# Values of four heads at once, with 512 columns, and output projections inside the recurrence

## The chip, the cores and the metric

The kernel runs on one core of a Trainium2 chip. The metric is the device time of one execution in microseconds (us). Five engines work beside each other, each through its own list of instructions in order: TensorE (PE in the profile; its weight loads PEld), VectorE (DVE), ScalarE (ACT), GpSimd (POOL) and SyncE (SP), which here only issues DMAs. An instruction that waits holds up all that stand behind it on its engine.

## The reference: what is computed

Two layers over 512 latent tokens of width 1024, with 256 context tokens. Layer 0 is a gated linear recurrence in both directions over 16 heads; layer 1 is a convolution module, which the change doesn't touch. In layer 0, cut down:

```
p = h @ w_in                       # 1024 x 10240, for latents h and context hc
q, v, zf, zb, gate = split(p, 5)
gf, kf = log f, 1 - f   with f = lb + (1 - lb) * sigmoid(zf)       # the same for zb
sc = state after the context, from (kc, vc, gc)                    # per direction
S_t = diag(exp g_t) S_(t-1) + k_t^T v_t ;  o_t = S_t^T q_t         # per head, chunks of 16
y  = (rmsnorm(o_forward + o_backward) * silu(gate)) @ w_out
x  = x + gate_ada * y,   where shift, scale, gate_ada = split(silu(c) @ ada_w + ada_b, 3)
```

All is float32. The large products are made as three products of split numbers (a high part rounded to fp32r and the rest): high by high, low by high, high by low.

## The kernel before

After an opening that makes the modulated inputs `h_hi`, `h_lo` (and `hc` for the context), layer 0 runs over eight pairs of heads, `gi` = 0 to 7 (L607). A pair projects its forget gates (`proj_z`, tiles pz for the latents, pc for the context, weights wz), its queries (`proj_silu`, pq, wq), its values (`proj_values`, pv, wv) and its gates (pg, wg), and, in the pairs that `OUT_SETS` names (L42), adds the output projection of finished heads to the stream (`out_proj`, tiles op, weights wo). Then come the pair's two heads: `gla` (L321) makes the decays, the state S and the scores, up to the output o, and `readout` (L527) normalises and gates it. `gla` is a generator: its first part ends behind the state updates (L424, L427), its second at the output products (L517 to L525). After a pair come some of 32 pieces of the ada product (`ada_piece`, L161; the table in L685 gives each pair 4, 4, 4, 3, 3, 3, 3 and none): a piece is one load `adb` and eight VectorE instructions that sum into `adacc`, and a small matmul `adbps`.

The order on each engine is made by a scheduler from the program's order, the dependences and the free buffers of the pools, so products of the next pair stand among the steps of the heads of the pair before.

Weights come through `wpiece` (L196): SP loads 512 KB into a tile with the tag `raw`, ScalarE makes the high half (tag `whi`), VectorE the low half (`wlo`). `ada_piece` takes its `adb` from the same tag `raw`. The pool has three buffers of it (`wpool`, L75), so a load waits until the third load before it has been used up by both engines. PSUM tiles of products (`pj`) have three buffers.

The values of a pair take 2 weight pieces of 4 x 256, then for each of 6 token tiles (4 of latents, 2 of context) 24 matmuls of 256 columns (L304, L305, L308) and one copy to SBUF by ScalarE (L603). The last pair (`gi` = 7) has an order of its own (L624 to L637) and ends with the output projections of heads 10 to 13 and of heads 14 and 15.

## Time and profile before

| | us |
|---|---|
| median of 3 timed runs | 1325.85 (1321.75 to 1326.63) |
| profiled execution | 1325.56, span 1323.5 |
| mean granted TensorE clock | 0.991 |
| TensorE busy | 1288.8 (97%) |
| VectorE busy | 934.4 (71%) |
| ScalarE busy | 608.2 (46%) |
| GpSimd busy | 304.3 (23%) |
| memory traffic | 120.22 MB, 91 GB/s |

Busy time is the time in which an engine has an instruction under way; matmuls overlap, so the mean length of one (284 ns for one with 256 columns) is more than the distance from one to the next. The granted clock is a share of 2.4 GHz; at 0.50 TensorE runs at 1.2 GHz. A row in which an instruction ends with x8 holds eight of them. Names of tiles have their numbers left out, so h_o is any head's output.

### The profile page before, as it was taken

How to read it: one execution, taken by the hardware profiler on the slowest of the kernel's cores; microseconds unless marked ns; L12 is line 12 of the kernel's file. 1: busy time of each engine (PE TensorE's matmuls, PEld its weight loads, DVE VectorE, ACT ScalarE, POOL GpSimd, SP SyncE). 2: the span in 40 equal slices, each digit the busy share in tenths (PEclk: the TensorE clock that was granted, in tenths of full speed). 3: DMA queues.
4: the chain of work that ended last, by engine and by line, in shares of the span. 5: the costliest groups of instructions: out<-in, count | busy, mean ns of one | idle time of the engine just before them, and what ended most of it. 6: DMA issues, size and time to landing. Idle time of an engine off the chain costs nothing.

```text
span 1323.5 us, 19786 instructions
## 1 busy us (share of the span) xinstructions
PE 1288.8 (97%) x7956; PEld 1087.4 (82%) x7956; DVE 934.4 (71%) x1513; ACT 608.2 (46%) x920; POOL 304.3 (23%) x289
## 2 busy tenths in 40 slices
PE   6999999999999999999999999999999999999997
PEld 2698898888889888889889889876877778788887
DVE  6667987796787888687689788865666576574233
ACT  4355564552464354565256455524423233385331
POOL 2231330330231151151024033104212112112121
PEclk8999999999999999999999999999999999999999
DMA  9322113114112312213311311213433333123321
GB/s 352 156 80 79 51 49 128 49 49 159 54 47 77 128 49 77 84 49 97 112 36 62 122 39 48 75 48 108 135 103 122 120 96 119 64 80 96 96 80 64
DMA packets 36188, 120.22 MB, mean 91 GB/s; under 512 B 4643, under 2 KB 7107, under 8 KB 36097
## 3 DMA queue, kind: packets, MB, share of 16 engines
q1 hardware_dynamic: 35104, 115.79, 26.0%
q0 software_dynamic: 992, 3.18, 1.1%
q8 instruction: 62, 1.02, 0.3%
q14 instruction: 30, 0.24, 0.1%
HBM read 116.85 MB, written 2.10 MB: 90 GB/s over the span
## 4 chain that ended last, share of the span: by engine, by line
PE 77%; DVE 13%; ACT 4%; DMA 3%; issue 2%; POOL 1%; SPq 0%; DVEq 0%; ACTq 0%
PE pa L734 4%; PE pa L735 4%; PE pa L739 4%; PE pz L293 3%; PE pz L294 3%; PE pz L296 3%; PE op L563 2%; PE cop L876 2%; PE cop L880 2%; PE op L565 2%; PE op L564 2%; PE cop L877 2%; PE pgt L803 2%; PE pgt L801 2%; PE pgt L800 2%; PE py L773 2%
## 5 line engine op out<-in xcount | busy, mean ns | idle before, releaser
L734 PE MATMUL pa<-ci_hi,h_hi 128*128 128x512 f32 x256 | 100.3, 403 | 1.9 <-ACT h_hi L682 1.9
L735 PE MATMUL pa<-ci_lo,h_hi 128*128 128x512 f32 x256 | 99.7, 393 | 0.0
L293 PE MATMUL pz<-h_hi,wz_hi 128*128 128x512 f32 x232 | 92.1, 397 | 1.4 <-ACT wz_hi L136 1.4
L294 PE MATMUL pz<-h_lo,wz_hi 128*128 128x512 f32 x232 | 91.7, 395 | 0.0
L116 POOL TENSOR_SCALAR sg<-sg 128x1536 f32<-128x1536 f32 x16 | 75.6, 4726 | 63.6 <-ACT sg L582 63.3
L167 DVE SCALAR_TENSOR_TENSOR adacc<-adb,sc,adacc 128x128 f32<-128x128 f32 x224 | 76.9, 357 | 3.8
L424 DVE SCALAR_TENSOR_TENSOR h_S<-h_S,h_dec,h_kb 128x128 f32<-128x128 f32 x96 | 59.0, 614 | 27.1 <-ACT h_kb L418 26.0
L136 ACT ACTIVATE ci_hi<-ci_raw 128x1024 fp32r<-128x1024 f32 x29 | 30.8, 1061 | 102.2 <-PE pa L739 57.9
L138 POOL TENSOR_TENSOR ci_lo<-ci_raw,ci_hi 128x1024 fp32r<-128x1024 f32 x18 | 44.2, 2461 | 129.2 <-ACT ci_hi L136 102.9
L739 PE MATMUL pa<-ci_hi,h_lo 128*128 128x512 f32 x224 | 70.9, 392 | 0.0
L510 POOL TENSOR_TENSOR h_A<-a,a 128x512 f32<-128x512 f32 x16 | 36.6, 2290 | 129.8 <-DVE a L491 108.0
L304 PE MATMUL pv<-wv_hi,h_hi 128*128 128x256 f32 x256 | 63.3, 284 | 0.0
L305 PE MATMUL pv<-wv_hi,h_lo 128*128 128x256 f32 x256 | 63.3, 284 | 0.0
L296 PE MATMUL pz<-h_hi,wz_lo 128*128 128x512 f32 x232 | 60.7, 396 | 0.0
L734 PEld LDWEIGHTS pa<-ci_hi,h_hi 128*128 128x128 f32 x256 | 48.7, 190 | 14.1 <-issue 4.1
L136 ACT ACTIVATE wz_hi<-wz_raw 128x1024 fp32r<-128x1024 f32 x29 | 30.7, 1057 | 63.6 <-DMA wz_raw<-in_w_in 54.7
L294 PE MATMUL pc<-hc,wz_hi 128*128 128x256 f32 x232 | 59.1, 288 | 0.0
L293 PE MATMUL pc<-hc,wz_hi 128*128 128x256 f32 x232 | 58.8, 287 | 0.0
L735 PEld LDWEIGHTS pa<-ci_lo,h_hi 128*128 128x128 f32 x256 | 48.7, 190 | 11.5 <-issue 1.4
L138 DVE TENSOR_TENSOR wz_lo<-wz_raw,wz_hi 128x1024 fp32r<-128x1024 f32 x29 | 35.5, 1223 | 31.1 <-ACT wz_hi L136 30.7
L876 PE MATMUL cop<-zhi,co_hi 128*128 128x512 f32 (+1 forms) x160 | 54.2, 352 | 0.0
L369 POOL TENSOR_TENSOR h_ref<-h_tot,h_gt 128x64 f32<-128x64 f32 x16 | 16.8, 1048 | 160.5 <-DVE h_ref L396 157.3
(332 smaller groups left out, 3862.1 us busy)
## 6 DMA issues: line engine op xcount, KB each, us to landing
adb<-in_ada_c SPq DMA_DIRECT2D x32, 512.0 KB, 3.2
ci_raw<-in_c_in SPq DMA_DIRECT2D x32, 512.0 KB, 3.2
wz_raw<-in_w_in SPq DMA_DIRECT2D x29, 512.0 KB, 3.2
ada<-in_ada_a SPq DMA_DIRECT2D x16, 512.0 KB, 10.2
wv_raw<-in_w_v SPq DMA_DIRECT2D x16, 512.0 KB, 3.2
wg_raw<-in_w_in SPq DMA_DIRECT2D x16, 512.0 KB, 3.2
cg_raw<-in_c_gate SPq DMA_DIRECT2D x16, 512.0 KB, 3.2
co_raw<-in_c_out SPq DMA_DIRECT2D x16, 512.0 KB, 3.6
```

The source lines that it names most:

```text
L116: (G if pool_min else V).tensor_scalar(out=t, in0=t, scalar1=EMAX, scalar2=None, op0=ALU.min)
L138: lo_eng.tensor_tensor(out=lo, in0=raw, in1=hi.bitcast(F32), op=ALU.subtract)
L167: V.scalar_tensor_tensor(out=acc, in0=raw[:, k, :], scalar=sc[:, k, 0:1], in1=acc, op0=ALU.mult, op1=ALU.add)
L293: mm(ps[:, :T], lhsT=hi[:, k, :], rhs=rhi[k], start=(k == 0), stop=False)
L294: mm(ps[:, :T], lhsT=hi[:, k, :], rhs=rlo[k], start=False, stop=False)
L296: mm(ps[:, :T], lhsT=lo[:, k, :], rhs=rhi[k], start=False, stop=(k == KD - 1))
L304: mm(ps[:, :256], lhsT=lhi[k][:, c], rhs=hi[:, k % 4, :], start=(k == 0), stop=False)
L305: mm(ps[:, :256], lhsT=llo[k][:, c], rhs=hi[:, k % 4, :], start=False, stop=False)
L734: mm(pss[t], lhsT=h_hi[:, 2 * kq + k, c], rhs=hi[:, k, :], start=(kq == 0 and k == 0), stop=False)
L735: mm(pss[t], lhsT=h_hi[:, 2 * kq + k, c], rhs=lo[:, k, :], start=False, stop=False)
L739: mm(pss[t], lhsT=h_lo[:, 2 * kq + k, c], rhs=hi[:, k, :], start=False, stop=(kq == 3 and k == 1))
L876: mm(ps, lhsT=hi[:, i, c], rhs=zhi[ct][:, tok], start=(ct == 0), stop=False)
```

## The change

Values are made for four heads at a time: `proj_values(qi)` stands in the even pairs only, loads 4 weight pieces of 2 x 512, makes for each of the 6 token tiles 24 matmuls of 512 columns (the context's tiles first, and the three products of a k block next to each other), and copies each PSUM tile out in two halves of 256 columns, one to the value tile of each of the two pairs. The gates (pg) are projected ahead of the values. The output projections now cover heads 0 to 3, 4 to 7 and 8 to 11 in the pairs 2, 4 and 6, written after the first part of the pair's first head instead of ahead of its heads; in the last pair heads 12 and 13 remain, then 14 and 15 as before. Copies of the split weights get 4 buffers instead of 3 (`W_BUFS`), of which the opening uses one more. The layout of w_v changes on the host's side of the inputs, and the program's scratch for dynamic DMAs is set to 8192. The number of output products (384), of their weight loads (20) and of the value weights' loads (16 of 512 KB) is what it was. Lines of the changed kernel stand one or two off from those of the kernel before.

```diff
--- before.py
+++ after.py
@@ -37,9 +37,10 @@
 RX_BUFS, RX_ENG, WE_ENG = 3, (0, 0, 1, 0, 0, 1, 0, 0), (1, 1, 0, 0, 0)
 CTX_MOD = ((), (), (0, 1, 2, 3, 4, 5), (6, 7))
 LAST_KQ = 1
+W_BUFS = 4
 FINAL = ((0, 2, 1), (2, 4, 0), (4, 6, 0))
 SET_LN_EXP, SET_SILU = 6, 18
-OUT_SETS = {2: (0, 1, 2, 3), 3: (4, 5), 5: (6, 7, 8, 9)}
+OUT_SETS = {2: (0, 1, 2, 3), 4: (4, 5, 6, 7), 6: (8, 9, 10, 11)}
 
 C_RESET = 0
 C_PRE = C_RESET + L
@@ -196,7 +197,7 @@
     def wpiece(src, shape, name, lo_eng, hi_eng=None):
         raw = wpool.tile([P] + shape, F32, name=f"{name}_raw", tag="raw")
         nc.sync.dma_start(out=raw, in_=src)
-        return split(wpool, raw, shape, name, lo_eng, ("whi", "wlo"), 3, hi_eng)
+        return split(wpool, raw, shape, name, lo_eng, ("whi", "wlo"), W_BUFS, hi_eng)
 
 
     with l0:
@@ -254,7 +255,7 @@
                     V.tensor_tensor(out=t, in0=x_sb[:, k, :], in1=rs, op=ALU.mult)
                     modulate(t, k, mod_g[:, k, 0:1], mod_s[:, k, 0:1], hx_hi, hx_lo)
                 for i in range(len(early), min(EARLY, len(early) + EARLY_LOADS[jj])):
-                    pool, tags, bufs = (wpool, ("whi", "wlo"), 3) if i < 3 else (pi, ("ehi", "elo"), EARLY - 3)
+                    pool, tags, bufs = (wpool, ("whi", "wlo"), W_BUFS) if i < W_BUFS else (pi, ("ehi", "elo"), EARLY - W_BUFS)
                     w = split(pool, wraws[i], [KD, P], f"we{i}", (V, G)[WE_ENG[i]], tags, bufs)
                     pspool, tag = (ps_p, "pj") if i < 3 else (ps_s, "sc")
                     early.append((w, pspool.tile([P, 512], F32, name=f"pe{i}", tag=tag)))
@@ -300,12 +301,10 @@
             ps = ps_p.tile([P, 512], F32, name=name, tag="pj")
             c = slice(t * P, (t + 1) * P)
             for k in range(KD):
-                hi, lo = ws[k // 4]
-                mm(ps[:, :256], lhsT=lhi[k][:, c], rhs=hi[:, k % 4, :], start=(k == 0), stop=False)
-                mm(ps[:, :256], lhsT=llo[k][:, c], rhs=hi[:, k % 4, :], start=False, stop=False)
-            for k in range(KD):
-                hi, lo = ws[k // 4]
-                mm(ps[:, :256], lhsT=lhi[k][:, c], rhs=lo[:, k % 4, :], start=False, stop=(k == KD - 1))
+                hi, lo = ws[k // 2]
+                mm(ps, lhsT=lhi[k][:, c], rhs=hi[:, k % 2, :], start=(k == 0), stop=False)
+                mm(ps, lhsT=llo[k][:, c], rhs=hi[:, k % 2, :], start=False, stop=False)
+                mm(ps, lhsT=lhi[k][:, c], rhs=lo[:, k % 2, :], start=False, stop=(k == KD - 1))
             return ps
 
         def silu_of(ps, t, name):
@@ -592,16 +591,18 @@
             silu_of(ps, t, f"{tag}{gi}_{j}")
             return t
 
-        def proj_values(gi):
-            ws = [wpiece(w_v[gi, kh], [4, 256], f"wv{gi}_{kh}", V) for kh in range(2)]
-            v = pt.tile([P, 6, 256], F32, name=f"v{gi}", tag="v", bufs=2)
-            for t in range(6):
+        def proj_values(qi):
+
+            ws = [wpiece(w_v[qi, kq], [2, 512], f"wv{qi}_{kq}", V) for kq in range(4)]
+            vs = [pt.tile([P, 6, 256], F32, name=f"v{qi}_{i}", tag="v", bufs=2) for i in range(2)]
+            for t in (4, 5, 0, 1, 2, 3):
                 if t < NB:
-                    ps = proj_v(ws, hx_hi, hx_lo, t, f"pv{gi}_{t}")
+                    ps = proj_v(ws, hx_hi, hx_lo, t, f"pv{qi}_{t}")
                 else:
-                    ps = proj_v(ws, hc_hi, hc_lo, t - NB, f"pv{gi}_{t}")
-                act(out=v[:, t, :], in_=ps[:, :256], func=AF.Copy)
-            return v
+                    ps = proj_v(ws, hc_hi, hc_lo, t - NB, f"pv{qi}_{t}")
+                for i in range(2):
+                    act(out=vs[i][:, t, :], in_=ps[:, i * 256:(i + 1) * 256], func=AF.Copy)
+            return vs
 
         m1 = cpool.tile([P, KD], F32, name="m1")
         for gi in range(8):
@@ -612,20 +613,22 @@
             if gi < 7:
                 sgs = [proj_z(gi, j) for j in range(2)]
                 qss = [proj_silu(0, gi, j, "q") for j in range(2)]
-                v = proj_values(gi)
                 gss = [proj_silu(4, gi, j, "g") for j in range(2)]
-                if gi in OUT_SETS:
-                    out_proj(OUT_SETS[gi])
+                if gi % 2 == 0:
+                    vs = proj_values(gi // 2)
+                v = vs[gi % 2]
                 for j in range(2):
                     parts = gla(h + j, j, sgs[j], qss[j], v)
                     next(parts)
+                    if j == 0 and gi in OUT_SETS:
+                        out_proj(OUT_SETS[gi])
                     readout(h + j, next(parts), gss[j])
             else:
                 sg, qs = [], []
                 for j in range(2):
                     sg.append(proj_z(gi, j))
                     qs.append(proj_silu(0, gi, j, "q"))
-                v = proj_values(gi)
+                v = vs[1]
                 parts = [gla(h + j, j, sg[j], qs[j], v) for j in range(2)]
                 next(parts[0])
                 next(parts[1])
@@ -634,7 +637,7 @@
                 readout(h, po, gs[0])
                 po = next(parts[1])
                 readout(h + 1, po, gs[1])
-                out_proj([10, 11, 12, 13])
+                out_proj([12, 13])
 
                 xg = [pt.tile([P, 3, L], F32, name=f"xg{i}", tag="sg", bufs=2) for i in range(2)]
                 xg = [xg[k // 3][:, k % 3, :] for k in range(6)]
@@ -938,7 +941,7 @@
     d["ada_c"] = np.concatenate([ada_w[0][:, 2 * D:], ada_w[1]], axis=1).reshape(KD, P, 32, P).transpose(2, 1, 0, 3)
     d["lb_logits"] = hgrn_lb_logits[:, 0].reshape(2, NH, P).transpose(2, 0, 1)
     d["w_in"] = hgrn_w_in[0].reshape(KD, P, 5, 8, 2, P).transpose(2, 3, 4, 1, 0, 5)
-    d["w_v"] = hgrn_w_in[0][:, E2:2 * E2].reshape(2, 4, P, 8, 256).transpose(3, 0, 2, 1, 4)
+    d["w_v"] = hgrn_w_in[0][:, E2:2 * E2].reshape(4, 2, P, 4, 512).transpose(3, 0, 2, 1, 4)
     d["hnorm_g"] = hgrn_norm_g[0].reshape(P, 1)
     d["w_out"] = hgrn_w_out[0].reshape(NH, P, 4, 256).transpose(2, 1, 0, 3)
     ci = conv_w_in[0].reshape(4, 2, P, 3, 4, 512)
@@ -957,7 +960,7 @@
     from concourse.bass_utils import run_bass_kernel_spmd as _run
 
     arrays = {f"in_{k}": v for k, v in _layout(**{k: np.asarray(v) for k, v in inputs.items()}).items()}
-    nc = _bacc.Bacc("TRN2", target_bir_lowering=False, num_devices=1)
+    nc = _bacc.Bacc("TRN2", target_bir_lowering=False, num_devices=1, dynamic_dma_scratch_size=8192)
     args = [nc.dram_tensor(k, v.shape, mybir.dt.from_np(v.dtype), kind="ExternalInput").ap() for k, v in arrays.items()]
     args.append(nc.dram_tensor("out_0", (P, KD, L), F32, kind="ExternalOutput").ap())
     with tile.TileContext(nc, schedule_with_timeline_sim=True) as tc:
```

The first place is TensorE before the first product of pair 2 (pz2_00, with the weights wz2_00). In these names pv1_5 is the last value tile of pair 1, pg1_0 and pg1_1 are pair 1's gates, adbps an ada piece's sum, and h2_ the small steps of head 2. Before:

```order
L308 MATMUL pv1_5_1834<-wv1_0_lo_1695,hc0_111 128x256 x4
L308 MATMUL pv1_5_1834<-wv1_1_lo_1701,hc1_112 128x256 x4
L293 MATMUL pg1_0_1866<-h_hi_81,wg1_0_hi_1862 128x512
...
L296 MATMUL pg1_1_1904<-h_hi_81,wg1_1_lo_1902 128x512 x8
L346 MATMUL h2_ct_1952<-kc_85,h2_ec_1944 128x128 x4
...
L413 MATMUL h2_kt0_2000<-kc_85,h2_kb_1993 128x128 x3
...
L293 MATMUL pz2_00_2369<-h_hi_81,wz2_00_hi_2365 128x512
```

The pair's value products stand ahead of its gates, and behind head 1's output. In the changed kernel the same place reads:

```order
L523 MATMUL h1_o_1316<-h1_qh_1214,h1_S_1181 128x128 x2
L294 MATMUL pg1_0_1716<-h_hi_81,wg1_0_hi_1712 128x512
...
L297 MATMUL pg1_1_1754<-h_hi_81,wg1_1_lo_1752 128x512 x8
L170 MATMUL adbps1_1369<-ones_94,adacc1_1360 128x1
L170 MATMUL adbps2_1383<-ones_94,adacc2_1374 128x1
L474 MATMUL h2_s0d_1890<-h2_qh_1841,h2_kl0_1888 64x64 x8
...
L170 MATMUL adbps3_1397<-ones_94,adacc3_1388 128x1
L345 MATMUL h2_ct_1802<-kc_85,h2_ec_1794 128x128 x4
...
L416 MATMUL h2_pp0_1855<-v0_1_811,h2_kb_1843 128x128 x3
L412 MATMUL h2_kt1_1863<-kc_85,h2_kb_1843 128x128 x3
L294 MATMUL pz2_00_2219<-h_hi_81,wz2_00_hi_2215 128x512
```

No value products are left between head 1's output and pz2_00: only the gates' products and head 2's small ones. The second place is VectorE at the end of ada piece 5 (adacc5), whose load stands three loads ahead of wz2_00's. Here wz2_00_lo is the low half of those weights, gs1_ are pair 1's gates, a1_0 the scores that the masked copies fill, and h3_ec belongs to head 3. Before:

```order
L165 TENSOR_SCALAR adacc5_2322<-adb5_2320,sc_100 128x128
L167 SCALAR_TENSOR_TENSOR adacc5_2322<-adb5_2320,sc_100,adacc5_2322 128x128 x4
L317 TENSOR_TENSOR gs1_0_1891<-gs1_0_1891,g1_0_e_1892 128x512
L167 SCALAR_TENSOR_TENSOR adacc5_2322<-adb5_2320,sc_100,adacc5_2322 128x128 x3
L313 TENSOR_SCALAR gs1_1_1929<-pg1_1_1904 128x512
L440 TENSOR_TENSOR h2_kl0_2038<-h2_kh_1992,h2_f16_1986 128x512
L336 SCALAR_TENSOR_TENSOR h3_ec_2129<-ones_94,h3_gt_2124 128x255
L338 SCALAR_TENSOR_TENSOR h3_ec_2129<-ones_94,h3_gt_2124 128x255
L138 TENSOR_TENSOR wz2_00_lo_2367<-wz2_00_raw_2363,wz2_00_hi_2365 128x1024
L491 COPY_PREDICATED a1_0_116<-masks_115,h2_s0d_2040 64x4x64 x2
```

and in the changed kernel:

```order
L312 TENSOR_SCALAR gs1_1_1779<-pg1_1_1754 128x512
...
L439 TENSOR_TENSOR h2_kl0_1888<-h2_kh_1842,h2_f16_1836 128x512
...
L490 COPY_PREDICATED a1_0_116<-masks_115,h2_s0d_1890 64x4x64 x2
...
L166 TENSOR_SCALAR adacc5_2172<-adb5_2170,sc_100 128x128
L168 SCALAR_TENSOR_TENSOR adacc5_2172<-adb5_2170,sc_100,adacc5_2172 128x128 x2
L457 COPY_PREDICATED a1_0_116<-masks_115,h2_sx_1892 128x512
L168 SCALAR_TENSOR_TENSOR adacc5_2172<-adb5_2170,sc_100,adacc5_2172 128x128 x5
L335 SCALAR_TENSOR_TENSOR h3_ec_1979<-ones_94,h3_gt_1974 128x255
L337 SCALAR_TENSOR_TENSOR h3_ec_1979<-ones_94,h3_gt_1974 128x255
L341 SCALAR_TENSOR_TENSOR h3_ec_1979<-sg1_1_1517,h3_ec_1979 128x512
L139 TENSOR_TENSOR wz2_00_lo_2217<-wz2_00_raw_2213,wz2_00_hi_2215 128x1024
```

Steps of head 2 that stood behind ada piece 5 (the copies into a1_0, the gate gs1_1 and kl0) now stand ahead of its end. From head 1's last state update to the end of the piece the list has 61 instructions before and 71 in the changed kernel; to the end of ada piece 12 behind head 5 it has 66 there, and to that of ada piece 18 behind head 9 it has 62. On SP the third place reads, in the changed kernel:

```order
L164 DMA adb4_2156<-in_ada_c 128x1024
L164 DMA adb5_2170<-in_ada_c 128x1024
L164 DMA adb6_2184<-in_ada_c 128x1024
L164 DMA adb7_2198<-in_ada_c 128x1024
L199 DMA wz2_00_raw_2213<-in_w_in 128x1024
L199 DMA wz2_10_raw_2271<-in_w_in 128x1024
...
L199 DMA wg2_1_raw_2560<-in_w_in 128x1024
L199 DMA wv1_0_raw_2598<-in_w_v 128x1024
```

The pieces adb4 to adb7 stand ahead of wz2_00 as they did before; the value weights (wv1 holds heads 4 to 7) moved behind the gates' weights.

## Rows read from the trace of the kernel before

**Rows 1.** The page: busy time by engine; granted clock in 40 slices.
```profile
PE 1288.8 (97%) x7956; PEld 1087.4 (82%) x7956; DVE 934.4 (71%) x1513; ACT 608.2 (46%) x920; POOL 304.3 (23%) x289
...
PEclk8999999999999999999999999999999999999999
```

**Rows 2.** Windows between two heads' last output products, columns in the first line.
```profile
core 0: us, PE busy (x) PEld busy (x) DVE busy (x) ACT busy (x) POOL busy (x), PEclk, DMA share, GB/s
185.60:237.40 51.80, 51.11 (x394) 46.22 (x394) 42.41 (x87) 23.24 (x40) 6.81 (x13) 1.00 0.28 92
394.40:462.00 67.60, 67.60 (x472) 59.53 (x471) 53.85 (x104) 30.80 (x51) 6.80 (x13) 1.00 0.31 102
597.40:675.70 78.30, 78.30 (x532) 69.40 (x530) 54.50 (x95) 31.73 (x49) 7.28 (x13) 1.00 0.29 95
809.70:876.40 66.70, 66.26 (x453) 60.69 (x452) 53.18 (x92) 32.12 (x55) 9.44 (x13) 1.00 0.17 52
```

**Rows 3.** Timeline of DVE (start, length, instruction): head 1's state, ada piece 5.
```profile
181.19 0.34 DVE L424 SCALAR_TENSOR_TENSOR h_S<-h_S,h_dec,h_kb 128x128 f32<-128x128 f32 x1
...
210.51 1.12 DVE L167 SCALAR_TENSOR_TENSOR adacc<-adb,sc,adacc 128x128 f32<-128x128 f32 x3
```

**Rows 4.** Chain of waits (start, length, what): products, a weight load.
```profile
188.07 0.96 PE pv L308 x8
...
205.33 1.81 PE pg L296 x8
...
217.64 3.20 DMA wz_raw<-in_w_in
```

**Rows 5.** Timeline of ACT: the high half of pair 2's first weights.
```profile
215.15 1.05 ACT L136 ACTIVATE wz_hi<-wz_raw 128x1024 fp32r<-128x1024 f32 x1
```

**Rows 6.** Timeline of PE: head 1's output, first product of wz2_00.
```profile
185.30 0.61 PE L524 MATMUL h_o<-h_qh,h_S 128*128 128x128 f32 x4
...
217.79 0.50 PE L293 MATMUL pz<-h_hi,wz_hi 128*128 128x512 f32 x1
```

**Rows 7.** Groups of value products: count | busy us, mean ns | idle before.
```profile
L304 PE MATMUL pv<-wv_hi,h_hi 128*128 128x256 f32 x256 | 63.3, 284 | 0.0
...
L304 PE MATMUL pv<-wv_hi,hc 128*128 128x256 f32 x128 | 31.7, 284 | 0.0
```

**Rows 8.** Window of the value tiles alone: length, PE, PEld, ACT busy.
```profile
185.60:217.80 32.20, 15.48 (x122) 14.94 (x122) 2.28 (x6) 1.00 0.30 99
```

**Rows 9.** Groups by line and form on DVE, columns as in rows 7.
```profile
L450 DVE TENSOR_TENSOR h_kl<-h_kh,h_fac 128x256 f32<-128x256 f32 x64 | 26.0, 463 | 0.0
...
L491 DVE COPY_PREDICATED a<-masks,h_s0d 64x256 f32<-64x256 uint8 x56 | 24.8, 444 | 6.4 <-PE h_s0d L475 5.1
...
L138 DVE TENSOR_TENSOR wg_lo<-wg_raw,wg_hi 128x1024 fp32r<-128x1024 f32 x16 | 19.5, 1217 | 0.9 <-PE pv L308 0.7
...
L440 DVE TENSOR_TENSOR h_kl<-h_kh,h_f 128x512 f32<-128x512 f32 x16 | 13.9, 871 | 0.0
...
L317 DVE TENSOR_TENSOR gs<-gs,g_e 128x512 f32<-128x512 f32 x16 | 11.0, 690 | 6.2 <-ACT g_e L316 6.2
L313 DVE TENSOR_SCALAR gs<-pg 128x512 f32<-128x512 f32 x16 | 10.9, 684 | 9.3 <-PE pg L296 9.2
...
L458 DVE COPY_PREDICATED a<-masks,h_sx 128x512 f32<-128x512 uint8 x14 | 10.4, 742 | 0.9
```

**Rows 10.** Window of PE alone, filled by head 2's small products.
```profile
212.60:217.80 5.20, 4.51 (x82) 1.00 0.30 101
```

**Rows 11.** Timeline of DVE: the last step of head 15's readout.
```profile
887.90 0.68 DVE L551 TENSOR_TENSOR h_ohl<-h_sq,h_ohl 128x512 fp32r<-128x512 f32 x1
```

**Rows 12.** Windows of PE in the opening: length, busy time, granted clock.
```profile
57.60:59.80 2.20, 0.37 (x2) 1.00 0.00 0
61.50:64.90 3.40, 3.37 (x8) 0.50 0.02 5
```

**Rows 13.** Waits of PE: us in total, times, longest.
```profile
PE pz L293 <- ACT wz_hi L136: 1.4, 1, 1.4
```

## The prediction

> **What bounds the kernel now.** I read the page's engine line first, then the windows between heads, then the chain of waits, and last single instructions around one boundary. TensorE is busy 1288.8 us of the 1323.5 us span, and its clock stands near full in nearly every slice [rows 1]; so work taken from TensorE shortens the run only where nothing else is late in its place. What nearly is late shows in the windows from the last output product of one head to that of the next: at heads 1 to 2, 5 to 6 and 9 to 10 TensorE is busy for 51.1 of 51.8, 67.6 of 67.6 and 78.3 of 78.3 us, while VectorE works 42.4, 53.9 and 54.5 us of the same stretches [rows 2]. VectorE is a second runner some 10 to 24 us behind, and the chain of waits already passes through it and the weight loads there.
>
> The link between the two is the `raw` buffers. Three of them serve all weight loads and the 32 ada pieces, and SP issues the loads in program order, ada pieces of a pair ahead of the next pair's first weights. Pair 2's first forget weights (wz2_00) therefore load only when VectorE has finished with ada piece 5. How close that is today: VectorE ends head 1's last state update at 181.53 and ada piece 5 at 211.63 [rows 3], 30.1 us later; the weights' load takes 3.2 us [rows 4] and their high half is ready at 216.20 [rows 5], 4.6 us behind the ada piece. TensorE, which ended head 1's output at 185.9, reaches the product that needs them at 217.79 [rows 6]: the weights are only 1.6 us early.
>
> **The change, part by part.** The sum stands against the profiled execution, 1325.56 us (span 1323.5; the median of the three timed runs is 1325.85, so both mean the same).
>
> *Value products.* Before: 1152 matmuls of 256 columns. The groups of 256 and of 128 in [rows 7] are the hi·hi ones, and the other two kinds have as many. Eight in a row take 0.96 us, 0.120 each; eight of 512 columns take 1.81 us, 0.226 each [rows 4]. After: 576 of 512 columns. 1152 x 0.120 = 138.2, 576 x 0.226 = 130.3: **-7.9**. If the denser window's mean for a value product, 15.48/122 = 0.127 [rows 8], held for all, the gain would be 16; if one of 512 columns cost two of 256, nothing. I take the two rows of eight, since they are runs of just these shapes. The Trainium skill, "TensorE: Matmul & The Clock Gate", section Back-to-back issue gap, gives an isolated gap of N/2.4 ns plus 2.5 ns; by it the whole saving would be an estimated 1.5 us, because wider products save only the fixed part. The rows' fixed part is larger than that, so the trace does not bear the formula out.
>
> *Where the values go.* They and the output projections are gone from the odd pairs, and it is in odd pairs that the three ada-gated loads come (pairs 1, 3 and 5 ahead of pairs 2, 4 and 6). The even pairs get the double.
>
> Boundary 1 to 2: of the 32.2 us from head 1's output to wz2_00's product, 122 value products go: 122 x 0.120 = 14.6 us [rows 8]. VectorE's list from the last state update to the end of ada piece 5 grows meanwhile from 61 to 71 instructions: more of head 2 is put ahead of the piece. Added are four kl of 0.463, four masked copies of 0.444, the two gate steps of 0.684 and 0.690, a kl of 0.871 and a masked copy of 0.742; two weight splits of 1.217 fall away [rows 9]: +4.2. So the wait is 14.6 - 1.6 + 4.2 = **17.2**. From the other side: 30.1 + 4.2 + 4.6 = 38.9 us after the state update the weights are there; TensorE has 4.4 us to head 1's end, 48 products of 512 columns (10.9) and head 2's small products (5.2 [rows 10]), 20.5 in all: 18.4. I keep 17.2.
>
> Boundary 5 to 6: the list to ada piece 12 has 66 instructions, and the mean of the stretch is 53.85/104 = 0.518 [rows 2]: 34.2, plus 4.6, is 38.8. TensorE has 4.4 + 87 x 0.226 + 5.2 = 29.3: **9.5**. Boundary 9 to 10: 62 x 54.50/95 (0.574) = 35.6, plus 4.6, is 40.2; TensorE 4.4 + 98 x 0.226 + 12 x 0.120 + 5.2 = 33.2: **7.0**. Together 33.7.
>
> That is the upper bound, since it lets VectorE's list keep the pace that it has now, idle time included or replaced by other work. The lower: VectorE idles 9.4 of 51.8, 13.8 of 67.6 and 23.8 of 78.3 us [rows 2]. If the lists of some 35 us close up by those shares, the weights come 6.4, 7.1 and 10.6 us sooner, and 10.8 + 2.4 + 0 = 13.2 us of waiting is left. Some of the idle is by TensorE's pace and goes (masked copies wait for products, [rows 9]); the rest is the head's own chain over ScalarE, which stays. I take **+28**, nearer the upper end, because 17.2 of it rests on a boundary where the slack was read directly.
>
> Even pairs: their stretches gain 15.3 us of values (144 x 0.226 - 144 x 0.120) and an output projection of 96 products (21.7 us). VectorE's work stays as it is, so TensorE stays last and no wait forms; what is queued there is in the sum already. The values need four weight pieces before the first product ends; the load behind them takes 3.2 us a piece against 24 products of 0.226 for a piece's share, so they are hidden: 0 (bounds 0 and 3 x 3.2).
>
> *Last pair.* In the last stretch (809.7 to 876.4) TensorE loses 144 value products (17.3 us) and half an output projection of 96 (48 x 0.226 = 10.8 us), VectorE has 53.2 of 66.7 us there [rows 2]. Head 15's readout then runs from 876.4 to 888.6 [rows 11]; the projection of heads 10 to 13 covers it today, and by the order about 5 us of the smaller one of heads 12 and 13 is left behind head 15's output. At most 12.2 - 5 = 7 is bare there, and another 3 in the stretch; at least 0, if the projection is late enough. **+4**.
>
> *Clock.* After a wait of 2.2 us TensorE's granted clock was 0.50, its 1.2 GHz level, for 3.4 us in which it did 8 products; later it is 1.00 again [rows 12]. Half of 3.4 is 1.7 lost. For the two longer waits: **+3.4** (0 to 5.1 with the third). The Trainium skill, same page, Part 1: The HAM clock gate, says that throttled is the default and activity releases it; that agrees with these rows, and would make every long wait cost more than its own length, as summed here.
>
> *Waits of before that go.* The one wait for wz_hi of 1.4 us [rows 13] lies where the even pair's products now stand: **-1.4** (0 to -1.4).
>
> *At nothing:* the 48 copies that bring values out of PSUM are as many and as wide as before (six took ScalarE 2.28 us, 0.38 each [rows 8]). A value tile's PSUM buffer is now held for two of them, 0.76 us, beside 24 products of 0.226 (5.4 us) into the next of three buffers: 0; bare, the second copies of 24 tiles would be 9.1. The fourth weight buffer can only let a split run earlier, and cannot let a load start, since `raw` still has three: 0 (0 to -3). The scratch size touches only POOL's DMA queue: 0 (plus or minus 1).
>
> Sum: -7.9 + 28 + 4 + 3.4 - 1.4 = **+26.1**, 1351.7: I say 1352.
>
> **Rivals.**
> *The waits don't come* (faster). Then only the values count: 1325.6 - 7.9 = 1318. For it: VectorE has time over in the lengthened even pairs and could run ahead of TensorE into the odd ones. Against: its list waits there for the head's own products and for `raw` buffers, and the odd pair's slack today is 1.6 us. Chance 0.08.
> *VectorE closes up:* waits 13.2, clock 1.7: 1325.6 - 7.9 + 13.2 + 4 + 1.7 - 1.4 = 1335. For it: its idle share [rows 2]. Chance 0.20.
> *The loads behind follow late too:* after the first weights each boundary waits once more for a load (3.2), since all pass the three `raw` buffers; with the upper waits, the last pair at 10 and the clock at 5.1: 1325.6 - 7.9 + 33.7 + 9.6 + 10 + 5.1 = 1376. Against: a piece's 24 and 24 products take 8.3 us, longer than load and split. Chance 0.14.
> *Forecast*, 0.58.
>
> **How the numbers follow.** The range takes the second rival in and ends just short of the third: 1332 to 1374. Within 0.5% (6.6 us, what a measurement of this kernel can tell) means 1319 to 1332: 0.03 of the first rival and 0.04 of the second's lower end; faster is the rest of the first, 0.05; slower 0.88.
>
> **What the profile after would show.** Three waits of TensorE at the forget product for the high half of its weights, of about 15, 8 and 5 us, behind the gate products of pairs 1, 3 and 5, with a dip of the granted clock behind the longer ones; 576 value products at 0.226; VectorE's busy time still about 934; TensorE's busy share down to about 95%. If the value products are cheaper and none of those waits stands there, the forecast is wrong by its largest term; if VectorE's list to ada piece 5 is not longer than 30 us, by half of it.

## The result and the profile after

The changed kernel takes 1382.28 us (median of 4 runs, 1380.92 to 1383.61) against 1325.41 us before: the ratio is 1.0424, 95% interval 1.0409 to 1.0438. The direction was forecast, the size not: 57 us slower where 26 were forecast, 8 us beyond the end of the range. The profiled execution has a span of 1381.6 us at a mean granted clock of 0.973.

The page's engine line and clock line, the answers to [rows 1]:

```profile
PE 1300.4 (94%) x7380; PEld 1069.8 (77%) x7380; DVE 921.0 (67%) x1513; ACT 610.1 (44%) x920; POOL 314.6 (23%) x289
...
PEclk9999998999999899999999999997999999999999
```

TensorE has 576 matmuls fewer and is busy for longer, because some of them run at half clock. The windows between the last output products of two heads, the answers to [rows 2], and behind them the stretch from head 15's output to the convolution's first product (columns as there):

```profile
196.70:247.30 50.60, 38.65 (x255) 33.15 (x254) 40.54 (x86) 19.32 (x32) 7.25 (x13) 0.87 0.22 64
419.20:480.50 61.30, 49.65 (x314) 42.13 (x314) 51.77 (x98) 28.54 (x44) 13.39 (x17) 0.89 0.27 86
638.70:694.50 55.80, 49.13 (x316) 41.72 (x315) 50.32 (x90) 30.12 (x47) 16.95 (x21) 0.94 0.23 68
860.80:926.30 65.50, 57.95 (x347) 50.93 (x346) 57.89 (x103) 32.71 (x56) 15.22 (x18) 0.95 0.18 53
926.30:961.20 34.90, 24.26 (x71) 13.96 (x69) 17.34 (x21) 14.84 (x25) 13.79 (x7) 0.84 0.16 50
```

Before, TensorE had no idle time to speak of in such stretches; now it is idle for 12, 11.7, 6.7, 7.6 and 10.6 us of them, at a lower clock, and the first stretch is hardly shorter than before (50.6 against 51.8 us) though it holds 18 us less work (33.5 at full clock against 51.1). The stretch from 876.4 to 906.6 was the last one's counterpart before, idle for 1.6 us:

```profile
876.40:906.60 30.20, 28.56 (x97) 18.29 (x96) 17.31 (x26) 15.30 (x27) 10.83 (x6) 0.94 0.29 94
```

The whole span can be divided so. For each window of 2 us, idle is its length less TensorE's busy time, "half clock" is busy time x (1 - granted clock), and what remains is work at full clock:

| us | before: idle, half clock | after: idle, half clock |
|---|---|---|
| start to head 1's output | 17.9, 3.2 | 17.4, 3.3 |
| the three odd boundaries (heads 1-2, 5-6, 9-10) | 0.7, 0 | 30.2, 12.2 |
| the other stretches up to head 13 | 4.9, 0 | 4.1, 0 |
| last pair (13-15) and on to the convolution | 1.8, 1.7 | 18.1, 7.0 |
| convolution layer | 9.3, 1.7 | 11.4, 2.5 |
| sum | 34.6, 6.6 | 81.2, 25.0 |
| work at full clock | 1282.3 | 1275.4 |

46.6 + 18.4 - 6.9 = 58.1, the difference of the two spans. Now the first boundary, instruction by instruction. VectorE (the answers to [rows 3]), ScalarE and TensorE (those to [rows 5, 6]), each start, length and instruction, in brackets the idle time before it:

```profile
191.39 0.34 DVE L423 SCALAR_TENSOR_TENSOR h_S<-h_S,h_dec,h_kb 128x128 f32<-128x128 f32 x1
...
222.73 1.89 DVE L168 SCALAR_TENSOR_TENSOR adacc<-adb,sc,adacc 128x128 f32<-128x128 f32 x5
```

```profile
228.13 1.06 ACT L137 ACTIVATE wz_hi<-wz_raw 128x1024 fp32r<-128x1024 f32 x1 [1.54 <-DMA wz_raw<-in_w_in]
```

```profile
205.91 1.98 PE L297 MATMUL pg<-h_hi,wg_lo 128*128 128x512 f32 x8
207.73 0.28 PE L170 MATMUL adbps<-ones,adacc 128*128 128x1 f32 x2
212.79 0.56 PE L170 MATMUL adbps<-ones,adacc 128*128 128x1 f32 x2 [4.79 <-DVE adacc L168]
215.29 1.12 PE L474 MATMUL h_s0d<-h_qh,h_kl 128*64 128x64 f32 x16 [1.94 <-DVE h_kl L439]
...
221.37 1.13 PE L355 MATMUL h_s<-v,h_ec 128*128 128x128 f32 x8 [1.22 <-DVE adac L172]
...
226.25 1.65 PE L416 MATMUL h_pp<-v,h_kb 128*128 128x128 f32 x6 [3.28 <-ACT h_kb L413]
...
229.24 0.80 PE L294 MATMUL pz<-h_hi,wz_hi 128*128 128x512 f32 x1 [0.71 <-ACT wz_hi L137]
```

From the state update's end (191.73) to the end of ada piece 5 (224.62) it is 32.9 us, and 4.6 us later, at 229.19, the weights are ready: TensorE starts on them at 229.24. It has nothing but pieces' sums and head 2's small products to run from 207.7 on. They stand ahead of pz in its order, so it takes its waits at them, a few us each, and only 0.71 at the weights. In this order the small products themselves end less than 1 us ahead of the weights, so this stretch alone does not tell which of the two holds TensorE up; the runs below do.

VectorE had little time over between a head's last state update and the end of the ada piece that the next weights wait for. Length, busy time and count at the first boundary before, then at the three after:

```profile
181.53:211.63 30.10, 26.86 (x62) 1.00 0.27 89
```

```profile
191.73:224.62 32.89, 29.62 (x72) 0.90 0.16 49
416.64:453.73 37.09, 33.75 (x68) 0.91 0.14 43
636.07:674.27 38.20, 33.77 (x64) 0.94 0.14 42
```

At the third boundary no wait for weights is left: their high half is ready at 678.81, and TensorE comes to them at 679.43, because it has stood still for ScalarE's step of the next head ahead of them:

```profile
669.30 1.52 PE L355 MATMUL h_s<-v,h_ec 128*128 128x128 f32 x8 [4.24 <-ACT h_ec L346]
```

Three products of the value group in a row (TensorE's timeline) start 0.23 us apart:

```profile
117.81 0.39 PE L305 MATMUL pv<-wv_hi,h_hi 128*128 128x512 f32 x1
118.04 0.39 PE L306 MATMUL pv<-wv_hi,h_lo 128*128 128x512 f32 x1
118.26 0.39 PE L307 MATMUL pv<-wv_lo,h_hi 128*128 128x512 f32 x1
```

The granted clock around the first boundary (windows: length, busy time, clock), beside [rows 12]:

```profile
212.00:218.00 6.00, 3.27 (x52) 0.55 0.31 90
218.00:226.00 8.00, 3.74 (x37) 0.91 0.49 140
226.00:233.00 7.00, 6.04 (x18) 0.52 0.38 130
```

### The profile page after: what moved, and what is told of

The parts are those of the page before. It is cut to its first block, busy times and chain, and to the rows that moved or that the text cites. A ratio compares the mean times of both kernels' runs of the same rounds, so it can differ in the third digit from the quotient of the medians.

```text
span 1381.6 us, 18594 instructions
## 1 busy us (share of the span) xinstructions
PE 1300.4 (94%) x7380; PEld 1069.8 (77%) x7380; DVE 921.0 (67%) x1513; ACT 610.1 (44%) x920; POOL 314.6 (23%) x289
## 5 line engine op out<-in xcount | busy, mean ns | idle before, releaser
L168 DVE SCALAR_TENSOR_TENSOR adacc<-adb,sc,adacc 128x128 f32<-128x128 f32 x224 | 80.4, 377 | 3.3
L139 DVE TENSOR_TENSOR wo_lo<-wo_raw,wo_hi 128x1024 fp32r<-128x1024 f32 (+1 forms) x20 | 20.6, 1030 | 63.6 <-ACT wo_hi L137 62.8
L509 POOL TENSOR_TENSOR h_A<-a,a 128x512 f32<-128x512 f32 x16 | 35.9, 2243 | 117.1 <-DVE a L490 77.2
L423 DVE SCALAR_TENSOR_TENSOR h_S<-h_S,h_dec,h_kb 128x128 f32<-128x128 f32 x96 | 43.0, 451 | 23.7 <-ACT h_kb L417 22.3
L294 PEld LDWEIGHTS pz<-h_hi,wz_hi 128*128 128x128 f32 x232 | 44.9, 194 | 12.8 <-ACT wz_hi L137 4.1
```

The source lines that it names most:

```text
L139: lo_eng.tensor_tensor(out=lo, in0=raw, in1=hi.bitcast(F32), op=ALU.subtract)
L168: V.scalar_tensor_tensor(out=acc, in0=raw[:, k, :], scalar=sc[:, k, 0:1], in1=acc, op0=ALU.mult, op1=ALU.add)
L294: mm(ps[:, :T], lhsT=hi[:, k, :], rhs=rhi[k], start=(k == 0), stop=False)
L423: V.scalar_tensor_tensor(out=S[:, d, dst, :], in0=S[:, d, src, :], scalar=dec[:, d, db:db + 1], in1=kb[:, d, pb * P:(pb + 1) * P], op0=ALU ...
```

## The experiments

All runs in one table. "Odd" is idle time plus half clock at the three odd boundaries, "end" the same from head 13's output to the convolution, "elsewhere" the rest of the span, "work" TensorE's at full clock, all from the profiled execution; the ratio is to the kernel before, with its 95% interval. Each edit also gives every engine another order of instructions, since the scheduler works it out anew (e10_scratch alone kept the order); a difference between two runs holds both.

| run | median | ratio | odd | end | elsewhere | work |
|---|---|---|---|---|---|---|
| before | 1325.4 | | 0.7 | 3.5 | 37.0 | 1282.3 |
| after | 1382.3 | 1.0424 (1.0409 to 1.0438) | 42.4 | 25.1 | 38.8 | 1275.4 |
| e1_values | 1368.1 | 1.0330 (1.0312 to 1.0348) | 29.1 | 24.5 | 39.5 | 1277.8 |
| e2_outproj | 1340.1 | 1.0114 (1.0099 to 1.0129) | 5.5 | 18.0 | 37.1 | 1279.8 |
| e9_small | 1340.1 | 1.0099 (1.0078 to 1.0120) | 2.7 | 4.0 | 49.5 | 1283.3 |
| e10_scratch | 1326.3 | 0.9995 (0.9984 to 1.0007) | 0.7 | 1.9 | 37.5 | 1281.8 |
| e12_early | 1341.2 | 1.0111 (1.0096 to 1.0127) | 2.8 | 3.8 | 52.0 | 1282.9 |
| e3_noload | 1347.7 | 1.0171 (1.0154 to 1.0188) | 15.5 | 22.6 | 35.3 | 1273.4 |
| e4_nosum | 1348.8 | 1.0173 (1.0152 to 1.0193) | 18.2 | 19.9 | 38.8 | 1272.6 |
| e6_fill | 1385.3 | 1.0443 (1.0423 to 1.0464) | 23.8 | 22.8 | 38.9 | 1296.6 |
| e7_tail | 1375.0 | 1.0373 (1.0358 to 1.0389) | 41.8 | 16.7 | 35.9 | 1276.2 |
| e8_lastpairs | 1357.7 | 1.0234 (1.0214 to 1.0254) | 28.5 | 3.9 | 43.4 | 1280.1 |
| e5_ada_even | 1381.5 | 1.0409 (1.0384 to 1.0434) | 6.5 | 17.2 | 84.3 | 1271.1 |
| b1 | 1390.6 | 1.0481 (1.0457 to 1.0504) | 13.2 | 5.0 | 89.5 | 1277.9 |
| b2 | 1342.0 | 1.0123 (1.0105 to 1.0142) | 15.7 | 4.2 | 41.0 | 1280.2 |
| c1_after_raw4 | 1369.3 | 1.0329 (1.0299 to 1.0359) | 34.7 | 24.1 | 33.8 | 1274.6 |
| c3_e8_raw4 | 1350.4 | 1.0191 (1.0169 to 1.0212) | 25.7 | 2.3 | 40.7 | 1280.3 |
| c2_b2_raw4 | 1330.9 | 1.0043 (1.0030 to 1.0056) | 10.5 | 2.5 | 35.7 | 1280.3 |
| b3_raw4 | 1317.1 | 0.9933 (0.9921 to 0.9945) | 0.3 | 2.3 | 30.5 | 1281.3 |
| b3_raw5 | 1319.0 | 0.9951 (0.9937 to 0.9965) | 0.2 | 2.0 | 35.7 | 1281.7 |

### The change taken apart

Values alone (the change without its output part):

```diff
-OUT_SETS = {2: (0, 1, 2, 3), 4: (4, 5, 6, 7), 6: (8, 9, 10, 11)}
+OUT_SETS = {2: (0, 1, 2, 3), 3: (4, 5), 5: (6, 7, 8, 9)}
...
+                if gi in OUT_SETS:
+                    out_proj(OUT_SETS[gi])
```

> The value half of the change alone: values of four heads with 512 columns in the even pairs, gates ahead of them, four weight buffers; the output projections stay in the sets and places of the kernel before (0-3 in pair 2, 4-5 in pair 3, 6-9 in pair 5, 10-13 at the end). Theory balance (TensorE runs dry in an odd pair when neither values nor an output projection are left there to cover the head's VectorE work): pair 1 stays dry and costs what it costs in the changed kernel, about 12 us idle and 5 us of half clock, pair 3 gets 10.9 us of products back and has about 1 us left, pair 5 has none, the end is as before: 1325 - 7 + 17 + 2, about 1337. Rival (the value products with 512 columns are themselves dearer in place, wherever the outputs stand): over 1360. Rival (outputs alone are to blame): about 1318.

Measured 1368: 31 us more than the balance gave. Pair 1 cost about what was said (18.6 with the clock), the other two boundaries 5 each where 1 in all had been expected; the larger part of the miss, 21 us, is the end, 24.5 us where 3.5 had been taken over from before. That the values, too, had covered the end was not seen. The time lies in the range of the rival with dearer value products, but they are not dearer: TensorE's work at full clock fell by 4.5 us.

Outputs alone (the new sets and place, on the kernel before):

> The output half alone: sets 0-3, 4-7, 8-11 in the pairs 2, 4 and 6 behind the first part of the pair's first head, 12-13 at the end; values as before, two heads at a time with 256 columns in every pair. Theory balance: odd pairs keep 17.3 us of values each, and VectorE was idle 13.8 and 23.8 us in the stretches that lose 10.9 and 21.8 us of outputs, so at most 1 to 2 us of waiting there; the end loses its cover and costs as in the changed kernel, about 17 us more idle and 5 us more of half clock: about 1345. Rival (the end's cost comes from the values made earlier, not from the smaller projection there): about 1326.

1340, near the balance's 1345: 4.8 us more at the boundaries, 14.5 at the end. Each half by itself bares most of the end, so the two don't add up there.

The small edits alone, and then each of them (the fourth buffer was run only with the smaller scratch):

```diff
+W_BUFS = 4
...
+    nc = _bacc.Bacc("TRN2", target_bir_lowering=False, num_devices=1, dynamic_dma_scratch_size=8192)
```

> The kernel before with only the fourth weight buffer and the scratch size of the changed kernel. Prediction: no change, 1326. Rival: the convolution layer, which took 416.6 us before and 420 to 423 in every run built from the changed kernel, pays for one of these two: about 4 us more, 1330.

> The kernel before with the scratch size alone: the same instructions in the same order on every engine. If the 13.5 us that the small edits cost come from the scratch itself (POOL's DMA queue), about 1339 with the same order; if they come from the fourth weight buffer, which changes the order, 1326.

> The small edits (scratch size, four weight buffers), but the opening's fourth weight stays in the opening's own pool, as in the kernel before. If the cost sits in the opening's use of the fourth buffer, about 1328; if it is spread over the heads because loads and splits of weights are ordered otherwise, it stays: about 1338.

The small edits cost 13.5 us, which neither the prediction nor this expectation had; the rival's 4 us in the convolution (420.1 against 416.6) are only a part. The scratch alone costs nothing, with the same order of instructions; keeping the opening's weight out of the fourth buffer gives nothing back. So the fourth pair of split buffers does it, and with it comes another order of instructions: 15 us of idle time and half clock more, 12.5 of them outside the boundaries and the end, in many waits of 1 to 3 us. Which part of the order costs them was not tried. The list of waits names head steps that come late from ScalarE (here of e9_small; line, releaser, us in total, times, longest):

```profile
PE h_pp L418 <- ACT h_kb L415: 3.9, 2, 3.0
...
PE h_kt L414 <- ACT h_S L358: 3.6, 3, 2.1
```

### What holds the odd boundaries up

No loads of the ada pieces (`raw = h_hi` in their place):

> The changed kernel, in which ada pieces 0 to 23 load nothing and read the modulated inputs instead of their weights (their sums are not the reference's); VectorE's work on them stays the same, and the three raw buffers serve weights alone. Theory gate (the next pair's first weights wait for an ada piece in a raw buffer, so TensorE has nothing but the head's own chain to run): the waits in pairs 1, 3 and 5 vanish, 30 us idle and 12 us of half clock: about 1340, with TensorE going from the gates straight into the next pair's forget products. Rival VectorE-bound (an odd pair's VectorE work is simply longer than TensorE's): the list on VectorE is as long, so most of the 30 us stays, at the head's products or one pair later: 1365 to 1380.

The sums cut short instead (k over `range(1, 1)` for the pieces of layer 0):

> The changed kernel, in which ada pieces 0 to 23 are loaded but only one of their eight parts is summed (the sums are not the reference's): 168 VectorE instructions of 0.357 us, 60 us of work in layer 0, are left out, and the raw buffers come free as soon as that one is done. Both theories take the waits at the odd boundaries away. Gate alone (VectorE otherwise has time): as without the loads, about 1348. VectorE's work in the odd pairs limits as well: the 12 us idle that stayed there without the loads goes too, and part of the waits at the end of the layer, 1325 to 1340.

Without the loads the odd boundaries fall from 42.4 to 15.5 us, though VectorE's list is as long; TensorE goes straight from pair 1's gates to the next pair's forget products (its timeline in e3_noload):

```profile
205.46 1.98 PE L300 MATMUL pg<-h_hi,wg_lo 128*128 128x512 f32 x8
207.28 0.39 PE L297 MATMUL pz<-h_hi,wz_hi 128*128 128x512 f32 x1
```

That is the gate: a load that waits for an ada piece, which stands at the end of a list of 33 to 38 us on VectorE. With 168 of VectorE's instructions left out and the loads kept (its busy time falls from 921.0 to 877.6 us, not by the 60 of the expectation) the boundaries fall to 18.2: no further. So cutting either link takes most of the wait away, and VectorE's length by itself is not the bound. Both times (1347.7 and 1348.8 us) are near what the gate alone gave in the expectations. It is worth some 27 of the 42.4 us: 11.7, 11.0 and 4.4 at the three boundaries. What is left, some 15 us, hangs on neither of the two alone. In e3_noload's list of waits it is steps of the heads on all three other engines: at the first boundary 3.6 us for GpSimd's h_A, at the second 1.5 and 1.3 for VectorE's h_kl and h_ol, at the third 2.3 for ScalarE's h_kb. Which of them could be shortened was not tried.

Work put into the gap:

```diff
+                if part == 4 and gi in (1, 3):
+                    proj(w, hx_hi, hx_lo, L, f"px{gi}_{j}")
```

> The changed kernel with the gate products of pairs 1 and 3 made twice, the first time for nothing: 96 products of 512 columns more, 21.8 us of work for TensorE, placed where it runs dry. Theory clock (the half clock there is the price of the idle time): idle time at the two places falls from 23.5 to about 4, half clock from 9.4 to about 2, so with 21.8 us more work the kernel takes about 1377, less than without it. Rival (the half clock does not hang on the waits): idle goes, clock stays, about 1384. Rival (the waits simply move behind the added work): about 1400.

Measured 1385.3, against 1382.3 without it: 21.8 us of products cost 3 us: 8 us more than the clock theory said and some 15 less than if the waits had moved. The time is that of the rival in which the clock stays low (1384), but not the mechanism: in its windows of the two boundaries (columns as in the windows above)

```profile
193.90:239.20 45.30, 39.76 (x268) 33.71 (x267) 40.00 (x85) 17.41 (x30) 6.52 (x13) 0.92 0.18 60
419.20:488.10 68.90, 64.80 (x390) 54.55 (x389) 54.54 (x98) 30.30 (x47) 17.44 (x18) 0.95 0.23 77
```

idle time falls from 23.6 to 9.6 us and half clock from 9.4 to 4.8. The clock goes with the idle time; the idle time fell less than expected, by 14 us and not by 19.5. Adding work to keep the clock up does not pay.

### The end

Heads 10 and 11 given back to the last projection, in the changed kernel (`6: (8, 9)` and `out_proj([10, 11, 12, 13])`):

> The changed kernel with heads 10 and 11 given back to the last pair: pair 6 projects heads 8 and 9, the end heads 10 to 13 as before the change. Theory cover (head 15's readout and the last pair's chain stand bare because half of the projection left the end): idle time from 860 us on falls from 18.5 to about 3 and half clock from 7 to 2, the products are as many: about 1382 - 17 = 1365. Rival (the wait there is for the loads of the convolution's taps, which start late whatever is projected): at most 5 us less, 1377 or more.

And, in the run with values alone, pairs 6 and 7 with values of their own again:

```diff
+                if gi == 6:
+                    vs = [proj_pair(6)]
...
-                v = vs[1]
+                v = proj_pair(7)
```

> The run with the value half alone (outputs in the sets and places of before), but pairs 6 and 7 make their values each for itself with 256 columns again, so that the last pair has value products of its own. Theory cover: the end of layer 0 was bare because the last pair had no values left to run beside its recurrence, so its products of the output projection were used up early; with them back, about 14 us idle and 7 us of half clock go, and a quarter of the 8 us that 512 columns saved: 1368 - 21 + 2, about 1349. Rival (the end hangs on loads or on the readout alone): 1365 to 1370.

The first brings 7 us, not 17: the stretch of the last pair is filled, the one behind head 15 is not, since TensorE has run those products by then (the last ends at 912.95, head 15's output at 915.63). The two windows of e7_tail:

```profile
848.40:915.60 67.20, 64.40 (x387) 55.99 (x387) 60.65 (x102) 33.33 (x56) 15.01 (x15) 1.00 0.16 52
915.60:950.20 34.60, 24.29 (x70) 13.98 (x68) 16.91 (x21) 15.18 (x25) 13.78 (x7) 0.85 0.20 65
```

That is a little more than its rival allowed (5 us); the wait of 4.3 us for the convolution's taps, of which the rival speaks, is still there.

The second takes the end to 3.9 us, as before the change, and the wait for the taps is gone. The windows from head 15's output on, of e1_values and then of e8_lastpairs:

```profile
912.80:947.90 35.10, 25.58 (x68) 14.87 (x67) 18.04 (x21) 15.07 (x25) 13.80 (x7) 0.81 0.16 51
```

```profile
903.60:934.60 31.00, 27.25 (x95) 16.66 (x93) 19.91 (x26) 16.20 (x27) 13.79 (x7) 0.96 0.28 92
```

So the last pair's own value products are what leaves the projection for the readout: behind head 15's output stand 25 products of the projection of heads 10 to 13 in e8_lastpairs, as before the change, and none in e1_values. The total stayed 9 us above the expectation: 4 of that are idle time and half clock elsewhere, and the profiled run of e1_values, from which it was worked out, lay almost 5 us above its median.

### Versions meant to be better

Pieces of the odd pairs moved into the even ones: all eight in a row behind the values (e5_ada_even; b1 has pairs 6 and 7 restored too), or only the odd pairs' seven, ahead of the values (b2):

```diff
+ADA_SETS = {2: (4, 5, 6, 7), 4: (12, 13, 14), 6: (18, 19, 20)}
...
+                for col in ADA_SETS.get(gi, ()):
+                    ada_piece(ada_c[col], col)
```

> The changed kernel with the 24 ada pieces of layer 0 moved: eight each behind the value products of pairs 0, 2 and 4 and ahead of those pairs' heads, none behind the odd pairs. Theory gate: the first weights of pairs 2, 4 and 6 no longer wait for a piece, and the pieces' 23 us of VectorE work lie beside the 32.5 us of value products: idle time at the three odd boundaries falls from 30 to the 12 us or less of the run without ada loads, half clock there from 12 to 3, the end as in the changed kernel: about 1355. Rival (the wait moves with the pieces into the even pairs, whose values, output weights or next weights then wait for them): 1375 or more.

> The run with pairs 6 and 7 restored, and in it the ada pieces moved behind the values of pairs 0, 2 and 4 as well. Theory gate and cover together: the 25 us that idle time and half clock still take at the three odd boundaries fall to about 5: about 1329, equal to the kernel before within 0.5%, with 6 us of products less. Rival (VectorE-bound): odd pairs stay as long as their VectorE work, 1340 or more.

> The run with pairs 6 and 7 restored, and only the seven ada pieces of the odd pairs moved: 4 to 7, 12 to 14 and 18 to 20 now stand ahead of the value products of pairs 2, 4 and 6; the others stay behind pairs 0, 2, 4 and 6. Unlike in the run with eight pieces in a row, the small products of the pieces stand between value products on TensorE, which does not wait for them. Theory gate and cover: idle and half clock at the three odd boundaries fall from 28 to about 6, the even stretches get no new wait: 1358 - 22, about 1336. Rival (any piece in an even pair costs there what it saves): 1355 or more.

Eight in a row free the odd boundaries (42.4 to 6.5 us) and lose more in the even stretches and the opening (elsewhere 38.8 to 84.3): as the rival had it, the wait moves with the pieces. TensorE waits there for their sums above all (waits of e5_ada_even):

```profile
PE adbps L171 <- DVE adacc L169: 31.3, 9, 4.6
```

b1 loses in the same way and missed its 1329 by 62 us. b2, where value products stand between the pieces, gets 16 of the 22 us. With a fourth `raw` buffer, for which the scratch is cut (4096 where split buffers are four, 8192 otherwise; 4096 was not timed by itself):

```diff
-        raw = wpool.tile([P] + shape, F32, name=f"{name}_raw", tag="raw")
+        raw = wpool.tile([P] + shape, F32, name=f"{name}_raw", tag="raw", bufs=4)
```

> The changed kernel, nothing left out, with a fourth raw buffer (room from a scratch of 4096): the next pair's first weights then wait for the fourth load before them, and so for an ada piece earlier. Theory gate: the odd boundaries lose a good part of the 30 us idle and 12 us of half clock, as they did without ada loads (1348); one buffer is one piece, some 3 us of VectorE work and one load of 3.2, at each of the weights of the three pairs: about 1360. Rival (what stands still is VectorE's own list, the buffers don't matter): 1378 to 1385.

> The best mixture so far with values of four heads in pairs 0 to 5 (pairs 6 and 7 restored, the odd pairs' ada pieces moved, 1342), with a fourth raw buffer. Theory gate: a further 8 us, as it gave the kernel before: about 1334, so that values with 512 columns still don't pay. Rival: the order without gated loads lets the 6 us of saved products through: below 1317.

> Values of four heads in pairs 0 to 5, pairs 6 and 7 restored, ada pieces where they were (1358), with a fourth raw buffer. Theory gate: the 28 us at the odd boundaries fall by more than half, as in the run with the pieces moved: about 1340. Rival (VectorE's own list): 1355 or more.

> The kernel before with the scratch size of the changed one and, in the room that this frees, a fourth raw buffer instead of a fourth pair of split buffers: a load then waits for the fourth load before it, no longer the third. Theory gate: before, the weights were just in time, so little is to be gained; 3 us of waits of TensorE on weights and ada pieces could go: 1323 to 1327. Rival (any new order costs some 10 us, as with the fourth split buffer): 1332 or more.

> The same with five raw buffers. Theory gate: as with four, 1322 to 1327. Rival (a new order costs): 1332 or more.

One more buffer takes 13 us off the changed kernel, 8 of them at the odd boundaries (22 had been expected in all), and 11 off b2 (8 expected). It takes 7 off e8_lastpairs, where 18 had been expected, and the odd boundaries there fall only from 28.5 to 25.7. Only on the kernel before does it end below it: b3_raw4, 1317.1 us, is faster than both kernels, by 9 us than before (0.9933, 0.9921 to 0.9945), more than was expected. There the gain is not at the odd boundaries, which had 0.7 us to lose, but in the other stretches (elsewhere 37.0 to 30.5). Its page:

```profile
PE 1285.9 (98%) x7956; PEld 1085.5 (83%) x7956; DVE 933.7 (71%) x1513; ACT 608.7 (46%) x920; POOL 302.6 (23%) x289
```

A fifth buffer adds nothing (1319.0).

## Why the prediction was wrong

*Value products, -7.9:* right within 1 us. Work at full clock fell by 6.9 us, products of 512 columns stand 0.23 us apart. The formula of the Trainium skill ("TensorE: Matmul & The Clock Gate", Back-to-back issue gap) for an isolated gap, by which it would have been an estimated 1.5, is not borne out by this work either.

*The odd boundaries, +28, and the clock, +3.4:* the place was right, and the mechanism for some 27 of 42.4 us (e3_noload). Idle time and half clock rose by 42.4 - 0.7 = 41.7 us where the two terms give 31.4. The prediction summed the time that TensorE loses up to the first product with the next pair's weights, and a dip of the clock behind it. Divided at that product, the windows of 2 us show 15.3, 14.3 and 9.5 us ahead of it (17.2, 9.5 and 7.0 were worked out) and 1.9, 1.6 and 0 us of half clock behind it. So the clock term came out as it was priced, 3.5 us, and it is the wait that was too small: 39.1 - 0.7 = 38.4 us against 28.

The step that failed there is the choice of 28 under a bound of 33.7, on the ground that VectorE's list would close up by its idle share. The shares taken were those of the whole windows (9.4 of 51.8 us and so on). In the stretch that counts, up to the end of the ada piece, VectorE was idle for only 3.2 of 30.1 us already before, and for 3.3, 3.3 and 4.4 us after: there was little to close up. Nor was 33.7 a bound: at the second and third boundary the list took 37.1 and 38.2 us where 34.2 and 35.6 had been counted. At the first the lists came out nearly as worked out (the weights were ready 37.5 us after the state update, 38.9 forecast), and TensorE had nearly 2 us more work than counted.

That the clock term came out is in part luck. Of the 12.2 us of half clock 8.7 lie ahead of that product, inside the wait, for the wait comes in pieces and the clock falls during it. And a dip is longer than the 3.4 us of [rows 12]: the windows above have 0.55 over 6 us and 0.52 over 7 us, but only a part of the second dip lies behind that product. The rule of the Trainium skill that was weighed there (same page, Part 1: The HAM clock gate: throttled is the default) agrees with these windows, 0.55 and 0.52 behind the waits and 0.91 between.

*The last pair, +4:* this is the term that failed most. Measured 25.1 - 3.5 = 21.6 us, 16.3 idle and 5.3 half clock. The step that failed is the cover behind head 15's output: the prediction counted about 5 us of the projection of heads 12 and 13 as left there, and none of it is. Its last product ends at 913.63, 13 us ahead of head 15's output; before, 25 products of the projection of heads 10 to 13 stood behind it, some 6 us. What stands there now is nine products of head 14's part of the last projection, 2.2 us, before TensorE waits 4.31 us for the convolution taps and then 2.10 for head 15's readout:

```profile
926.32 0.94 PE L562 MATMUL op<-h_ohl,wo_hi 128*128 128x512 f32 x3
...
928.49 1.02 PE L539 MATMUL h_ms<-h_sq,ones 128*128 128x512 f32 x2
933.83 3.73 PE L676 MATMUL wtp<-dw,tap 31*118 31x512 f32 x4 [4.31 <-DMA dw<-in_c_dw]
939.66 1.65 PE L562 MATMUL op<-h_ohl,wo_hi 128*128 128x512 f32 x3 [2.10 <-ACT h_ohl L549]
```

It had taken the 17.3 us of values out of the last stretch's sum and not asked what they had kept for later; e8_lastpairs shows that they were the cover. The taps are no later than they were: their first product runs 7.3 us behind head 15's output, 7.5 before the change. But the prediction named only the readout as what is bare, and the readout itself stands behind the taps: on VectorE its first step (h_sq) comes after a copy of their product, for which VectorE sits idle 12.02 us.

```profile
935.89 0.69 DVE L677 COPY wt<-wtp 118x512 f32<-118x512 f32 x1 [12.02 <-PE wtp L676]
936.50 0.68 DVE L547 TENSOR_TENSOR h_sq<-h_sq,h_o 128x512 f32<-128x512 f32 x1
```

Whether an earlier load of the taps would shorten the bare stretch was not tried.

*At nothing:* wrong for the fourth split buffer. With the kernel before's work it costs 13.5 us (e9_small), with another order of instructions. The changed kernel was not run without it. How much of the changed kernel's 57 it makes up is not settled: there the same idle time is counted under the boundaries and the end, and only the convolution layer's 2.9 us stand apart.

*Even pairs and the wait for wz_hi, -1.4:* the other stretches up to head 13 have 0.8 us less idle time: near enough.

Of the 32 us by which the sum fell short, 17.6 are the last pair's, 10.3 the boundaries' with their clock, 2.9 the convolution layer's and 1.0 the values'; the rest cancels.

The forecast said that TensorE would wait at the forget products for some 15, 8 and 5 us; it waits at the pieces and small products in front of them. Whoever looked only for a wait at the weights would find 3.3 us in the list of waits, the answer to [rows 13], and take the mechanism for refuted:

```profile
PE pz L294 <- ACT wz_hi L137: 3.3, 2, 2.6
```

The rival with late loads gave 1376 and had the total nearer, by other terms: no second wait for a load stands in the trace.

## What to carry to other kernels

Cheaper instructions are worth their saving only if the work stays spread: here 7 us less TensorE work came with 65 us of idle time and half clock, most of it because work left the stretches where it had covered another engine's chain (27 us at the gate, 21 at the end; how much the fourth split buffer adds is open). Before moving work, list for every stretch what it covers, the end above all; and look which shared buffer lets the next loads start, for that may be the cheaper thing to change (one `raw` buffer more: 9 us off the kernel before). When a list is said to close up, read its idle time in the stretch that counts, not in a wider window. A change of a buffer count is a change of the whole order and is to be timed by itself.

## What the runs showed of the hardware

TensorE's clock cost more than one dip suggested: with 46.6 us more idle time came 18.4 us more of half clock, and a run with less idle time at the same boundaries had less of both (23.6 and 9.4 us against 9.6 and 4.8). A wait of 4.79 us ended at 212.79; from 212 to 218 the granted clock was 0.55, over the 8 us behind that 0.91.

Idle time is not all that comes ahead of a dip. In the kernel before, TensorE was busy for all of the 2.5 us from 885.0 on, at the full 2.4 GHz, with the taps' products among others; then the clock fell to 0.51, near the level of 1.2 GHz, for 3.5 us:

```profile
885.00:887.50 2.50, 2.50 (x7) 1.00 0.58 193
887.50:891.00 3.50, 3.50 (x10) 0.51 0.04 14
```
